# Two output projections taken one token stream at a time, with the residuals and norms placed behind them

## The chip, the cores and the metric

The kernel runs on one core of a Trainium2 chip. The metric is device microseconds (us) for one execution, taken as the median of three runs. Every run below is of the same program on the same inputs.

## The reference, cut to what matters

Two layers run over two token streams of 256 tokens each, context (`ctx`, stream 0) and latent (`x`, stream 1), with 1024 channels. Only the latent stream is wanted at the end, so the second layer gives no context output. Of each layer this much matters here:

```python
sh1, sc1, g1, sh2, sc2, g2 = split(silu(c) @ ada_w[layer] + ada_b[layer], 6)   # one set per stream
u = rms_norm(h, g_pre1) * (1 + sc1) + sh1
...                                               # three token mixers, each projected and gated
y = merged @ w_out                                # (256 tokens of a stream, 1024) @ (1024, 1024)
h = h + g1 * rms_norm(y, g_post1)
v = rms_norm(h, g_pre2) * (1 + sc2) + sh2
a = silu(conv3(v @ w_gate)) * (v @ w_val)         # 2816 channels
h = h + g2 * rms_norm(a @ w_ffn_out, g_post2)     # (256, 2816) @ (2816, 1024)
```

All values are float32.

## The kernel before, in words

**Products.** A float32 operand is split into a high part of a reduced format, which ScalarE writes with a cast, and a low part, the remainder, which VectorE or GpSimd writes with a subtraction. A product is then three matmuls: high x high, high x low, low x high. `weights` does it for a chunk of 128 x 1024 weights: one DMA of 512 KB from the SP queue into one of 5 buffers `raw`, one cast (`wh`, ScalarE), one subtraction (`wl`, VectorE), with 3 buffers each for `wh` and `wl`. The casts and subtractions stand in a block of high priority.

**Order.** A scheduler orders each engine's instructions at compile time, by priority (the order in which the code emits them) and by when its own model finds them ready. At run time each engine takes them strictly in that order, and a waiting instruction holds up all behind it.

**The output projections.** `outputs` computes `wo` (8 blocks of 128 input channels) and `fo` (22 blocks). A result of 128 tokens x 512 columns fills one PSUM bank. There are 3 banks `mm` and 5 banks `ps`. In layer 0, `outputs` takes the first 512 columns for both streams together, so that a chunk of weights serves 24 matmuls, and then the second 512 columns stream by stream, where each chunk serves 12 and is loaded and split again for the other stream. Stream 0's activations in front of `fo` are kept unsplit. `inner` splits one block of them when it is asked for: a cast into `ah` on ScalarE (L1170) and a subtraction into `al` on GpSimd (L1171), 128 x 256 each, two buffers each. In `outputs` it is asked once for each block and each half, and both tiles of 128 tokens use the answer.

**Behind the projections.** `post_half` takes the sum of squares of a bank (ScalarE, L383) and multiplies it with the gain row (VectorE, L436). `post_end` finishes the norm with two small GpSimd operations (L441, L378) and adds to the residual `h` (VectorE, L442). `norm_in` takes the next norm of `h`: a square pass (ScalarE), two small GpSimd operations, and a scaling of half the columns on ScalarE (L394) and half on VectorE (L395), into `hn`. `prenorm` then transposes `hn` by blocks of 128 (TensorE, L405, at high priority) and writes the split result `act`: high part on ScalarE (L409), the value again on VectorE (L411) and the remainder on VectorE or GpSimd (L412), two blocks to a call. All this is emitted after the whole projection.

**Modulation.** What the next steps need of `silu(c) @ ada_w` comes in two ways. `ada_dots` loads 512 KB of `ada_w` transposed and takes one product-and-sum on VectorE (L338, a "dot") for each stream wanted. `ada_units` does it on TensorE with narrow matmuls (L289), two units of 32 (64 instructions in the trace each) in either layer behind `wo`. In layer 0, the dots after `wo` are taken 2.7 for each of the FFN's blocks, and the rest beside the first half of `fo`.

Of the kernel before, what the change touches and what calls it, by code (L numbers as in the profile page):

```python
# [170 lines left out]
class Net:  # L171
# [102 lines left out]
    def ada_unit(self, l, cols, raw=None):  # L274

        nc = self.nc
        bank = self.ps()
        acc = bank[:, :P]
        nj = sum(n for _, n in cols) // P
        kb = 8 // nj  # L280
        for k2 in range(0, KD, kb):
            r = (raw or self.raw)(1024).rearrange("p (k c) -> p k c", k=kb)
            at = 0
            for c0, n in cols:
                nc.sync.dma_start(r[:, :, at:at + n], self.d["ada"][l, k2 * P:(k2 + kb) * P, c0:c0 + n].rearrange("(k p) c -> p k c", p=P))
                at += n
            for k in range(kb):
                for j in range(nj):
                    nc.tensor.matmul(acc[32 * j:32 * j + 32, :], self.scol[:, k2 + k, :], r[:, k, j * P:(j + 1) * P],  # L289
                                     start=k2 + k == 0, stop=k2 + k == KD - 1, skip_group_check=True)  # L290
            yield 460
        self.ada_turn(l, cols, bank)

# [32 lines left out]
    def ada_units(self, l, units):  # L326
        return chain(*(self.ada_unit(l, ((512 * i, 512),)) for i in units))

# [14 lines left out]
    def weights(self, key, urgent=True):  # L343
        nc = self.nc
        at, n = self.woff[key]
        raw = self.raw(n)
        nc.sync.dma_start(raw, self.d["wflat"][at:at + P * n].rearrange("(p f) -> p f", p=P))
        with self.tc.high_priority() if urgent else nullcontext():
            h = self.wp.tile([P, WCH], F32R, tag="wh", name=self.nm("wh"))[:, :n]
            nc.scalar.copy(h, raw)  # L350
            lo = self.wp.tile([P, WCH], F32R, tag="wl", name=self.nm("wl"))[:, :n]
            nc.vector.tensor_sub(lo, raw, h.bitcast(F32))  # L352
        return h, lo
# [43 lines left out]
    def prenorm(self, tp, l, ms, hn, k, boff, dst):  # L397

        nc = self.nc
        ps = self.ps().rearrange("p (i c) -> p i c", i=2)  # L400
        todo = [(m, g) for m in ms for g in hn]
        with self.tc.high_priority():
            for i, (m, g) in enumerate(todo):
                for t in range(2):
                    nc.tensor.transpose(ps[:, i, t * P:(t + 1) * P], hn[g][t][:, m * P:(m + 1) * P], self.ident)  # L405
        for i, (m, g) in enumerate(todo):
# [4 lines left out]
            nc.vector.tensor_scalar(t, ps[:, i], a, b, ALU.mult, ALU.add)  # L411
            (nc.gpsimd if i % 2 else nc.vector).tensor_sub(dst[1][:, m, c], t, dst[0][:, m, c].bitcast(F32))  # L412

    def norm_in(self, tp, l, g, hs, k, boff, dst):
        hn = [tp.tile([P, D], F32, tag="yg", name=self.nm("hn"), bufs=4) for _ in hs]
        for t in range(2):
            self.scaled(hn[t], self.rms(hn[t], hs[t]), hs[t])
        for m in range(0, KD, 2):
            self.prenorm(tp, l, (m, m + 1), {g: hn}, k, boff, dst)
# [18 lines left out]
    def post_end(self, s, yg, h):  # L438
# [3 lines left out]
        self.nc.vector.scalar_tensor_tensor(h, yg, self.rstd(ms, 1), h, ALU.mult, ALU.add)  # L442

    def outputs(self, key, nk, x, tp, gains, order, fill=iter(())):

        y, part = {}, {}

        def half(i, gs):
            for g in gs:
                y[g] = [(self.mm if 2 * i + t < MM_BANKS and g == order[0] and len(order) > 1 else self.ps)() for t in range(2)]  # L450
            last = nk - (4 if i and (gs[0] or nk == KD) else 0)
            for k in range(0, last, 2):
                w = self.weights((*key, i, k))
                if i == 0:
                    next(fill, None)
                for j in range(2):
                    for g in gs:
                        x_ = x(g, k + j)
                        for t in range(2):
                            self.tokens_proj(y[g][t], [a[:, t * P:(t + 1) * P] for a in x_], [a[:, 512 * j:512 * j + 512] for a in w], k + j == 0, k + j == nk - 1)  # L460
            ws = [(k, self.weights((*key, i, k))) for k in range(last, nk, 2)]
            for t in range(2 if ws else 0):
                for k, w in ws:
                    for j in range(2):
                        self.tokens_proj(y[g][t], [a[:, t * P:(t + 1) * P] for a in x(g, k + j)], [a[:, 512 * j:512 * j + 512] for a in w], False, k + j == nk - 1)
            for g in gs:
                for t in range(2):
                    self.post_half(tp, y[g][t], gains[g], i, *part[g, t])

        for g in order:  # L470
            for t in range(2):
                part[g, t] = self.st(2), tp.tile([P, D], F32, tag="yg", name=self.nm("yg"), bufs=4)
        half(0, order)
        for g in order:
            half(1, (g,))
        return part
# [810 lines left out]
```

## Time and profile before

| | |
|---|---|
| median of three runs | 1566.59 us (1565.92 to 1570.48) |
| the profiled execution | 1565.92 us, of which the span of instructions is 1564.1 us |
| mean granted TensorE clock | 0.991 |
| TensorE (PE) busy | 1485.0 us, 95% of the span |
| VectorE (DVE) busy | 1039.7 us, 66% |
| ScalarE (ACT) busy | 737.6 us, 47% |
| GpSimd (POOL) busy | 244.6 us, 16% |
| read from HBM | 225.06 MB, 145 GB/s over the span |

Times of rows count from the span's start. A busy TensorE need not be at its best pace, since matmuls overlap: a matmul with 512 columns lasts about 0.39 us, and the next one starts well before it ends. So the distance between starts is what counts, and a stage is read by how many matmuls it holds and how long it takes.

### The profile page before, as it was taken

What the parts mean: (1) busy time and instruction counts of PE and PEld (TensorE: products, weight loads), DVE (VectorE), ACT (ScalarE), POOL (GpSimd) and SP (SyncE); (2) the same over time, 40 slices, a digit from 0 to 9 for tenths busy, and PEclk for the clock granted to TensorE, in tenths of its full rate; (3) what the DMA queues carried; (4) which work ended last, traced back from release to release, by engine and by line L of the source; (5) the groups of instructions that cost most, each with busy time, mean ns of one, the idle gap of its engine ahead of it and who ended that gap; (6) DMA issues with size and microseconds to landing.
All of it is one profiled execution on the core that took longest, in us unless ns stands there. A gap on an engine that the chain in (4) does not pass through costs nothing.

```text
span 1564.1 us, 24165 instructions
## 1 busy us (share of the span) xinstructions
PE 1485.0 (95%) x9187; PEld 1275.2 (82%) x9187; DVE 1039.7 (66%) x1872; ACT 737.6 (47%) x1326; POOL 244.6 (16%) x335
## 2 busy tenths in 40 slices
PE   6999989999999998999999999899999989899998
PEld 5889867777777887888878886899997878699986
DVE  5546677778897448777776447646667797577754
ACT  3463334454454346332323346564456555455543
POOL 2101220101211223000000316401111123100000
PEclk9999999999999999999999999999999999899999
DMA  9331134423332356766665544422351234655553
GB/s 355 115 95 61 61 121 128 139 71 95 109 120 87 116 174 217 233 238 217 227 207 174 171 138 158 127 95 82 95 166 65 75 108 122 215 187 185 185 182 105
DMA packets 69717, 227.70 MB, mean 146 GB/s; under 512 B 7712, under 2 KB 8368, under 8 KB 69600
## 3 DMA queue, kind: packets, MB, share of 16 engines
q1 hardware_dynamic: 68000, 220.76, 43.4%
q0 software_dynamic: 1600, 5.39, 1.0%
q8 instruction: 72, 1.18, 0.3%
q14 instruction: 45, 0.37, 0.1%
HBM read 225.06 MB, written 1.06 MB: 145 GB/s over the span
## 4 chain that ended last, share of the span: by engine, by line
PE 62%; DVE 14%; issue 7%; DMA 7%; ACT 5%; POOL 4%; SPq 0%; POOLq 0%; ACTq 0%; DVEq 0%
PE mm L364 8%; PE mm L365 8%; PE mm L366 8%; DMA raw<-in_adat 6%; DVE wl L352 4%; PE ps L483 4%; PE ps L481 4%; PE ps L482 4%; DVE adot L338 3%; POOL st L378 2%; PE ps L366 2%; PE mm L579 2%; PE ps L364 2%; PE ps L365 2%; PE mm L580 2%
## 5 line engine op out<-in xcount | busy, mean ns | idle before, releaser
L352 DVE TENSOR_TENSOR wl<-raw,wh 128x1024 fp32r<-128x1024 f32 (+6 forms) x333 | 386.3, 1165 | 185.5 <-ACT wh L350 184.4
L350 ACT CAST wh<-raw 128x1024 fp32r<-128x1024 f32 (+6 forms) x333 | 320.1, 966 | 245.8 <-PE mm L365 102.6
L364 PE MATMUL mm<-act,wh 128*128 128x256 f32 (+1 forms) x1096 | 372.6, 340 | 5.4 <-ACT sig L978 2.0
L366 PE MATMUL mm<-act,wl 128*128 128x256 f32 (+1 forms) x1096 | 370.4, 338 | 3.4 <-DVE wl L352 3.4
L365 PE MATMUL mm<-act,wh 128*128 128x256 f32 (+1 forms) x1096 | 370.3, 338 | 0.2 <-POOL act L412 0.2
L364 PEld LDWEIGHTS mm<-act,wh 128*128 128x128 f32 x1096 | 210.2, 192 | 27.8 <-ACT wh L350 3.6
L366 PEld LDWEIGHTS mm<-act,wl 128*128 128x128 f32 x1096 | 210.1, 192 | 25.3 <-DVE wl L352 4.6
L365 PEld LDWEIGHTS mm<-act,wh 128*128 128x128 f32 x1096 | 210.3, 192 | 20.1 <-POOL act L412 0.4
L338 DVE CUSTOM_DVE_ANT_0 adot<-raw,srow,S 128x1024 bf16<-128x1024 f32 x104 | 134.2, 1291 | 73.6 <-DMA raw<-in_adat 69.0
L366 PE MATMUL ps<-act,wl 128*128 128x256 f32 (+1 forms) x328 | 109.5, 334 | 1.1 <-DVE wl L352 1.1
L364 PE MATMUL ps<-act,wh 128*128 128x256 f32 (+1 forms) x328 | 109.4, 333 | 0.0
L365 PE MATMUL ps<-act,wh 128*128 128x256 f32 (+1 forms) x328 | 109.3, 333 | 0.0
L483 PE MATMUL ps<-wh,al 128*128 128x512 f32 x198 | 78.8, 398 | 3.2 <-POOL al L1171 3.2
L579 PE MATMUL mm<-wh,act 128*128 128x272 f32 (+1 forms) x256 | 77.7, 303 | 1.3 <-ACT kb L795 1.3
L1047 ACT ACTIVATE ft<-ft 128x256 f32<-128x256 f32 (+1 forms) x47 | 23.7, 503 | 114.2 <-DVE ft L1045 90.5
L581 PE MATMUL mm<-wh,act 128*128 128x272 f32 (+1 forms) x256 | 76.9, 301 | 0.3 <-POOL act L412 0.3
L580 PE MATMUL mm<-wl,act 128*128 128x272 f32 (+1 forms) x256 | 76.8, 300 | 0.3 <-DVE wl L352 0.3
L1171 POOL TENSOR_TENSOR al<-ac,ah 128x256 fp32r<-128x256 f32 x44 | 41.4, 944 | 214.5 <-ACT ah L1170 214.3
L366 PEld LDWEIGHTS ps<-act,wl 128*128 128x128 f32 x328 | 62.7, 191 | 7.5 <-DVE wl L352 1.5
L365 PEld LDWEIGHTS ps<-act,wh 128*128 128x128 f32 x328 | 62.7, 191 | 6.0
L364 PEld LDWEIGHTS ps<-act,wh 128*128 128x128 f32 x328 | 62.8, 191 | 5.8
L378 POOL TENSOR_TENSOR st<-st,mhalf 128x1 f32<-128x1 f32 (+3 forms) x56 | 48.6, 868 | 95.9 <-DVE st L606 59.0
(300 smaller groups left out, 2812.4 us busy)
## 6 DMA issues: line engine op xcount, KB each, us to landing
raw<-in_wflat SPq DMA_DIRECT2D x253, 512.0 KB, 3.6
raw<-in_adat SPq DMA_DIRECT2D x80, 512.0 KB, 4.2
raw<-in_wflat SPq DMA_DIRECT2D x48, 256.0 KB, 2.6
araw<-in_ada SPq DMA_DIRECT2D x16, 512.0 KB, 7.5
raw<-in_ada SPq DMA_DIRECT2D x16, 512.0 KB, 4.1
raw<-in_wflat SPq DMA_DIRECT2D x8, 480.0 KB, 3.5
raw<-in_wflat SPq DMA_DIRECT2D x8, 408.0 KB, 3.4
raw<-in_wflat SPq DMA_DIRECT2D x8, 384.0 KB, 6.6
```

The source lines that it names most:

```text
L338: nc.vector.tensor_tensor_reduce(junk, r, rows[:, i], 1.0, self.S[l][:, L_AB + b:L_AB + b + 1], ALU.mult, ALU.add, self.MV[l][:, b, g:g + 1])
L350: nc.scalar.copy(h, raw)
L352: nc.vector.tensor_sub(lo, raw, h.bitcast(F32))
L364: self.nc.tensor.matmul(ps, a, xh(k), start=first and k == 0, stop=False)
L365: self.nc.tensor.matmul(ps, a, xl(k), start=False, stop=False)
L366: self.nc.tensor.matmul(ps, b, xh(k), start=False, stop=last and k == nk - 1)
L378: self.nc.gpsimd.tensor_tensor(r, ms, self.mhalf[:, :n], ALU.pow)
L481: self.nc.tensor.matmul(ps, xh, wh, start=first, stop=False)
L483: self.nc.tensor.matmul(ps, xl, wh, start=False, stop=last)
L579: nc.tensor.matmul(ps, uh[:, k, tt], h[:, c], start=k == 0, stop=False)
L580: nc.tensor.matmul(ps, uh[:, k, tt], lo[:, c], start=False, stop=False)
L581: nc.tensor.matmul(ps, ul[:, k, tt], h[:, c], start=False, stop=k == KD - 1)
```

## The change: what it does

- `outputs` now serves one stream for a call. Without `split`, the loop runs over pairs of blocks, inside it over the two column halves, inside that over the tiles of 128 tokens of the group `ts`, so four banks (or two) fill at once. The activation block is asked for (`x(k + j)`) in the innermost loop, for each half and each tile.
- In layer 0, `wo` runs for stream 0 and then stream 1; `fo` for stream 1 and then stream 0. All weights of `wo` and `fo` are thus loaded and split once for each stream. In layer 1, `wo` runs by tiles of 128 tokens, with split weights kept in a pool of their own for the second tile; `fo` keeps its order, with both tiles one after the other for the last two chunks of the second half.
- `renorm` replaces `norm_in`: the residual is added by halves of 512 columns, and ScalarE squares each half as it is done. It is called as soon as a tile of 128 tokens has both its halves. `normed` and `normed_next` emit the transposes of a stream in the midst of the next stream's products (`mid`), the early FFN blocks or the next layer's first projections, and no longer at high priority.
- In `prenorm` the remainder is always on VectorE; the second block of a call has its value taken again on ScalarE.
- `ada_units` is gone. In layer 0, dots are taken 2.4 for each FFN block, and the remaining ones beside the first 16 weight chunks of `fo` for stream 1. In layer 1, 16 dots (shift and scale of the second norm) go beside the first and the third merge, and 8 (the last gate) beside the FFN.
- The last residual is added and stored by halves of 512 columns.

```diff
+    def renorm(self, tp, s, yg, h):
+        q, ms = self.st(2), self.st(1)
+        self.post_end(s, yg, h, lambda i, c: self.square_sums(tp.tile([P, 512], F32, tag="ft", name=self.nm("jq"), bufs=2), h[:, c], q[:, i:i + 1]))
+        self.nc.gpsimd.tensor_scalar(ms, q[:, 0:1], q[:, 1:2], EPS, ALU.add, ALU.add)
+        hn = tp.tile([P, D], F32, tag="yg", name=self.nm("hn"), bufs=4)
+        self.scaled(hn, self.rstd(ms, 1), h)
+        return hn
...
+        for ts in tiles:
+            y = {(t, i): (self.mm if t == 0 else self.ps)() for t in ts for i in range(2)}
+            for k in range(0, nk, 2) if ts[0] == 0 else (nk - 2, *range(0, nk - 2, 2)):
+                for i in range(2):
+                    w = weights(i, k)
+                    for t in ts:
+                        for j in range(2):
+                            first, last = (k + j == 0, k + j == nk - 1) if ts[0] == 0 else (k + j == nk - 2, k + j == nk - 3)
+                            self.tokens_proj(y[t, i], [a[:, t * P:(t + 1) * P] for a in x(k + j)], [a[:, 512 * j:512 * j + 512] for a in w], first, last)
+                if mid and k == mid[0]:
+                    mid[1]()
+            for t in ts:
+                for i in range(2):
+                    end(t, i, y[t, i])
+                done(t, *yg[t])
...
-            ada = self.ada_dots(ap, [(l, b) for b in range(16, 40)], (0, 1)) if full else iter(())
+            ada = self.ada_dots(ap, [(l, b) for b in range(16 if full else 24, 40)], (0, 1) if full else (1,))
...
-            run(self.merge(l, sp, u, 2, yC, acc, q0, nq, mg))
+            run(self.beside(self.merge(l, sp, u, 2, yC, acc, q0, nq, mg), ada, 3000))
...
-        part = self.outputs((l, "wo"), KD, lambda g, k: (mg[0][:, k, at(g)], mg[1][:, k, at(g)]), fp, rows, groups, gains())
+        if full:
+            wo(0)
+            wo(1, mid=(KD - 4, partial(normed, 0)))
+        else:
+            with pool("wo", far) as wp:
+                wo(1, wp=wp, tiles=((0,), (1,)))
+                turn(0)
+                turn(1)
         mst.close()
-        ada = chain(self.ada_units(l + 1, range(2)), *(self.ada_dots(fp, [(l, b) for b in range(40, 48)] + [(l + 1, b) for b in range(8, 40 if g else 16)], (g,)) for g in range(2))) if full else self.ada_units(l, range(10, 12))
+        second = [(l, b) for b in range(40, 48)]
+        ada = chain(*(dots(second + [(l + 1, b) for b in range(24 if g else 16)], g) for g in range(2))) if full else dots(second, 1)
...
-                due += 2.7 if j < NF - 2 else 0
+                due += (2.4 if full else 0.5) if j < NF - 2 else 0
...
-        part = self.outputs((l, "fo"), NF, inner, fp, rows, groups[::-1], ada)
+            fo(partial(inner, 1), fp, lambda: rows[1], fill=lambda k: next(ada, None), done=renormed(1))
+            run(ada)
+            fo(partial(inner, 0), fp, lambda: rows[0], mid=(14, partial(normed_next, 1)), done=renormed(0))
...
+        def store(t, s, yg):
+            self.post_end(s, yg, hs[1][t], lambda i, c: nc.sync.dma_start(self.d["out"][t * P:(t + 1) * P, c], hs[1][t][:, c]))
+        fo(partial(inner, 1), fp, lambda: rows[1], split=4, done=store)
```

## Rows read from the trace of the kernel before

**Rows 1.** The page: busy time, share of the span and instructions by engine.

```profile
PE 1485.0 (95%) x9187; PEld 1275.2 (82%) x9187; DVE 1039.7 (66%) x1872; ACT 737.6 (47%) x1326; POOL 244.6 (16%) x335
```

**Rows 2.** Windows: length; busy PE, PEld, DVE, ACT, POOL; granted clock; DMA share, GB/s.

```profile
541.90:642.20 100.30, 92.93 (x658) 79.67 (x657) 67.28 (x98) 55.38 (x92) 25.50 (x30) 1.00 0.60 195
852.80:983.60 130.80, 126.93 (x548) 99.78 (x547) 66.93 (x72) 63.21 (x109) 49.23 (x60) 1.00 0.49 157
983.60:1008.80 25.20, 20.64 (x161) 20.44 (x160) 18.32 (x29) 15.83 (x30) 10.52 (x17) 0.93 0.37 108
220.00:440.00 220.00, 211.03 (x1201) 169.62 (x1200) 175.13 (x374) 108.09 (x217) 30.02 (x29) 0.99 0.36 114
1150.00:1222.00 72.00, 67.78 (x566) 59.93 (x565) 52.07 (x114) 43.97 (x90) 9.33 (x11) 1.00 0.29 91
1325.30:1351.80 26.50, 24.85 (x109) 20.00 (x112) 15.38 (x18) 11.59 (x19) 3.98 (x5) 0.94 0.59 182
1351.80:1372.20 20.40, 14.20 (x174) 12.30 (x175) 13.64 (x26) 11.10 (x19) 5.72 (x9) 0.75 0.74 257
1372.20:1495.60 123.40, 123.40 (x1030) 123.40 (x1030) 87.00 (x129) 69.65 (x108) 0.74 (x1) 1.00 0.58 184
636.00:656.00 20.00, 19.79 (x110) 17.40 (x111) 17.06 (x28) 7.61 (x12) 0.00 (x0) 1.00 0.83 281
```

**Rows 3.** TensorE in order of time, where layer 0's `wo` ends.

```profile
586.49 0.40 PE L481 MATMUL ps<-wh,mg 128*128 128x512 f32 x1
...
588.36 0.40 PE L483 MATMUL ps<-wh,mg 128*128 128x512 f32 x1
588.69 2.15 PE L289 MATMUL ps<-raw,scol 128*32 128x128 f32 x66
590.77 1.56 PE L405 MATMUL ps<-ident,hn 128*128 128x128 f32 x12
```

**Rows 4.** TensorE in order of time, where layer 1's `wo` ends.

```profile
1351.39 0.39 PE L483 MATMUL ps<-wh,mg 128*128 128x512 f32 x1
...
1359.00 2.82 PE L405 MATMUL ps<-ident,hn 128*128 128x128 f32 x12 [0.81 <-DVE hn L395]
...
1364.59 0.38 PE L364 MATMUL mm<-act,wh 128*128 128x256 f32 x1 [0.73 <-ACT wh L350]
```

**Rows 5.** TensorE in order of time, at the start of layer 1.

```profile
993.16 0.56 PE L405 MATMUL ps<-ident,hn 128*128 128x128 f32 x2 [4.56 <-ACT hn L394]
```

**Rows 6.** Groups of instructions by form over the span: busy us, mean ns.

```profile
L352 DVE TENSOR_TENSOR wl<-raw,wh 128x1024 fp32r<-128x1024 f32 x253 | 320.6, 1270 | 157.3 <-ACT wh L350 156.8
L350 ACT CAST wh<-raw 128x1024 fp32r<-128x1024 f32 x253 | 264.4, 1047 | 196.8 <-PE mm L365 76.1 <-PE ps L483 60.0 <-PE ps L365 34.9
L338 DVE CUSTOM_DVE_ANT_0 adot<-raw,srow,S 128x1024 bf16<-128x1024 f32 x104 | 134.2, 1291 | 73.6 <-DMA raw<-in_adat 69.0 <-DMA srow<-sdram 4.0
L409 ACT ACTIVATE act<-ps,MV,A 128x256 fp32r<-128x256 f32 x56 | 29.6, 563 | 32.2 <-PE ps L405 21.4 <-DVE nt L411 10.8
L1171 POOL TENSOR_TENSOR al<-ac,ah 128x256 fp32r<-128x256 f32 x44 | 41.4, 944 | 214.5 <-ACT ah L1170 214.3
L378 POOL TENSOR_TENSOR st<-st,mhalf 128x1 f32<-128x1 f32 x26 | 17.5, 675 | 6.1 <-DVE st L1224 4.2
L441 POOL TENSOR_SCALAR st<-st 128x1 f32<-128x1 f32 x12 | 6.9, 572 | 262.7 <-ACT junk L383 262.5
```

**Rows 7.** Line 1171 alone: duration min/median/max, and what waited for it.

```profile
L1171 POOL TENSOR_TENSOR al<-ac,ah x44: 722/738/1814, 614.8 to 981.0; 128x256 fp32r<-128x256 f32 x44
```

**Rows 8.** GpSimd in order of time, in the last part of layer 0's `fo`.

```profile
973.88 2.15 POOL L1171 TENSOR_TENSOR al<-ac,ah 128x256 fp32r<-128x256 f32 x2 [0.22 <-ACT ah L1170]
...
978.32 0.74 POOL L1171 TENSOR_TENSOR al<-ac,ah 128x256 fp32r<-128x256 f32 x1 [0.30 <-ACT ah L1170]
```

**Rows 9.** The page: DMA issues, KB each, us from issue to landing.

```profile
raw<-in_adat SPq DMA_DIRECT2D x80, 512.0 KB, 4.2
```

**Rows 10.** VectorE in order of time, at the end.

```profile
1558.51 1.28 DVE L442 SCALAR_TENSOR_TENSOR hL<-yg,st,hL 128x1024 f32<-128x1024 f32 x1 [0.47 <-POOL st L378]
```

More of the change, by code (lines that the diff above doesn't have):

```diff
@@ L341, in ada_dots, with weights @@
             yield 1500
[L343 removed]
+    def weights(self, key, urgent=True, pool=None):
         nc = self.nc
@@ L395, in scaled, with turned, prenorm @@
         self.nc.vector.tensor_scalar_mul(dst[:, D // 2:], src[:, D // 2:], r)
[L397 removed]
+    def turned(self, ps, ms, hn, t):
+        for i, m in enumerate(ms):
+            self.nc.tensor.transpose(ps[:, i * SEQ + t * P:i * SEQ + (t + 1) * P], hn[:, m * P:(m + 1) * P], self.ident)
+    def prenorm(self, tp, l, ms, hn, k, boff, dst, ps=None):
         nc = self.nc
[L400 removed]
         todo = [(m, g) for m in ms for g in hn]
[L402 removed]
+        if ps is None:
+            ps = self.ps()
             for i, (m, g) in enumerate(todo):
                 for t in range(2):
[L405 removed]
+                    self.turned(ps[:, i * SEQ:], (m,), hn[g][t], t)
+        ps = ps.rearrange("p (i c) -> p i c", i=2)
         for i, (m, g) in enumerate(todo):
@@ L410, in prenorm @@
             t = tp.tile([P, SEQ], F32, tag="nt", name=self.nm("nt"), bufs=2)
[L411 to L419, printed above, removed]
+            if i % 2:
+                nc.scalar.activation(t, ps[:, i], AF.Identity, bias=b, scale=a)
+            else:
+                nc.vector.tensor_scalar(t, ps[:, i], a, b, ALU.mult, ALU.add)
+            nc.vector.tensor_sub(dst[1][:, m, c], t, dst[0][:, m, c].bitcast(F32))
     def gate_rows(self, fp, l, k, g):
@@ L436, in post_half, with post_end @@
         self.nc.vector.tensor_mul(yg[:, c], y, gain[:, c])
-    def post_end(self, s, yg, h):
+    def post_end(self, s, yg, h, after):
         ms = self.st(1)
         self.nc.gpsimd.tensor_scalar(ms, s[:, 0:1], s[:, 1:2], EPS, ALU.add, ALU.add)
[L442 to L466, printed above, removed]
-                for t in range(2):
[L468 to L476, printed above, removed]
@@ L1148, in layer @@
         for g in groups:
-            for t in range(2):
-                self.post_end(*part[g, t], hs[g][t])
-            self.norm_in(fp, l, g, hs[g], "A2", 24, v)
             for j in early:
                 self.ffn_pair(l, fp, j, v, new(j), g * CTX, CTX, q0, True, j >= 2)
+                if not g and j == early[-2]:
+                    normed(1)
+        if not full:
+            for i, ps in enumerate(turns):
+                self.prenorm(fp, l, (2 * i, 2 * i + 1), {1: hn[1]}, "A2", 24, v, ps)
         due = 0
```

115 lines of the change are left out of this document (72 added, 43 removed).

## The prediction, made before the changed kernel was run

> **What bounds the kernel now.** I read the page first: TensorE is busy 95% of the span and every other engine 66% or less [rows 1]. So the time is a sum of matmuls at their best pace plus the places where TensorE runs short. I then cut the span into stretches and compared each with the pace of its matmuls. In the FFN of layer 1, TensorE is busy for the whole 123.4 us and starts 1030 matmuls of 256 columns, one each 0.120 us [rows 2]. In `wo`, matmuls of 512 columns start 0.234 us apart (nine from 586.49 to 588.36), a transpose takes 0.13 us (twelve in 1.56), and a narrow matmul of `ada_units` 0.033 us (66 in 2.15) [rows 3]. With these prices each stretch that the change touches has an ideal length, and what lies above it is what the change can win.
>
> Layer 0 from `wo` to the end of the early FFN blocks takes 100.3 us [rows 2]. It holds 192 products (44.9), 16 transposes of gains (2.1), 32 of `hn` (4.2), 288 FFN matmuls (34.5) and 128 narrow ones (4.2): 89.9. So 10.4 us are waits. The border to layer 1 takes 25.2 us [rows 2] for 144 matmuls (17.3) and 16 transposes (2.1), 5.8 us too many, of which one wait for `hn` is 4.56 us [rows 5]. In layer 1 the last product of `wo` starts at 1351.39, and the last transposes begin at 1359.00 [rows 4]; the granted clock of the stretch behind it is 0.75 [rows 2], a mean of the two levels 2.4 and 1.2 GHz. The FFN's 1056 matmuls would take 126.5 us back from 1495.6, so it starts in effect at 1369.1, 17.3 us after `wo`.
>
> **Layer 0, `wo` and early FFN.** `ada_units` goes (-4.2). The 16 weight chunks, where there were 12, cost 1.05 us of ScalarE and 1.27 us of VectorE each [rows 6] under 12 products (2.8 us): hidden. If both are lost or delayed, TensorE waits. Stream 0's chain from the last product to `hn` took 7.2 us in layer 1, from 1351.8 to 1359.0 [rows 4]. It now has three quarters of the second `wo` (17 us) to run in. Stream 1's has two FFN blocks (11.5 us). Ideal is 85.7, so the gain lies between 4.2 (all waits stay) and 14.6 (none). The normalization of a stream puts 12 ScalarE passes of 0.53 us [rows 6] beside the FFN's casts, so I leave 3.6 us of waits: **-11**.
>
> **Border to layer 1.** Without priority the transposes of stream 0 no longer stand in front of ready projections. That gives at most 5.8. The first V product then needs stream 0 whole: 12 ScalarE passes (6.4 us) against some 4 us of transposes and products, so I give back 2.3: **-3.5**, from -5.8 to 0.
>
> **Layer 1, `wo` and its norm.** The second tile's chain stays: 7.2 us. The first tile's transposes go into it. Then four pairs of blocks at three ScalarE passes each (1.6 us) feed the first FFN product; the last pair is ready 0.5 + 6.4 us later, at 14.1, and the 2.9 us of that product end with it: the FFN starts in effect at 11.2, not 17.3. At the clock that the idle time leaves [rows 2] I take -5. Against it, a chunk now serves six products (1.4 us) in the first tile. Eight chunks and four dots left over come to 6.3 MB (512 KB each [rows 9]). Part is loaded under the last merge, which leaves VectorE and the DMA room; I take +2, at worst +11. Sum **-3**, from -8 to +6.
>
> **Dots in layer 1.** 16 dots are 21 us of VectorE at 1.29 us [rows 6]. Both ends: 0, and 21 if each delays the attention's chain. The stretch of the first merge has VectorE busy 52 of 72 us and TensorE 67.8 of 72; layer 0 carries its dots in 220 to 440, with TensorE busy 211 of 220 [rows 2], no worse. **+3**. The 8 dots under the FFN are free: VectorE is busy 87 of 123.4 us there [rows 2], and TensorE never waits.
>
> **Layer 0, `fo`: the decisive part.** It takes 130.8 us now [rows 2]. Products are 264 for each stream, 61.8 us. Stream 1: 61.8 plus 2 for the gains, plus what the dots cost. For 16 chunks, weights and dot ask for 1.05 MB in 2.8 us, 373 GB/s, where the fastest stretch shown with these buffers moved 281 [rows 2]. VectorE needs 2.6 of the 2.8 us [rows 6]. Three chunks split ahead and five loaded cover most: +3, from 0 to +15 (all at 281 GB/s).
>
> Stream 0 is where I expect the loss. `x(k + j)` is called in the innermost loop, and for stream 0 that is `inner`, which emits a cast and a GpSimd subtraction at each call. Before, 22 blocks x 2 halves are 44 calls [rows 6]. After, 22 x 2 halves x 2 tiles are 88, each serving three products, 0.70 us. A subtraction takes 0.944 us in the mean [rows 6] and 0.738 in the median [rows 7]. Two of them that meet a VectorE subtraction take 2.15 us [rows 8], 0.67 more than two medians. So GpSimd needs 88 x 0.738 = 64.9 us at the least, 79.7 if each of the 22 chunks costs 0.67 once, and 83.1 at the mean, against 61.8 of products. I take the mean, since the stage it comes from has the same chunks and casts. In the same queue stand two tiles' norms of stream 1, each two L441 and two L378 (2.5 us): 88. At worst a weight cast (1.05 us) also delays a subtraction in each chunk: 111. The other operations of `prenorm` and its transposes fall into TensorE's waits. `fo` is 61.8 + 2 + 3 + 88 = 154.8: **+24**, from -2 (64.9, dots free) to +59 (111, dots at +15).
>
> The Trainium skill, on the page "SBUF — State Buffer" (section "SBUF: two separate sides"), says that GpSimd shares a port pair with VectorE, as an exclusive lock: a VectorE operation with two SBUF inputs and a GpSimd operation that reads SBUF block one another for the whole instruction. By that rule each chunk would cost a whole `wl`. The trace shows a little over half (0.67 of 1.27 us).
>
> **The end.** Two half additions in place of one of 1.28 us [rows 10], each followed by its store. The last store starts as late as before: 0. FFN 0 with 40 dots in place of 45: 0.
>
> **Sum.** -11 - 3.5 - 3 + 3 + 24 = +9.5 against the profiled execution's 1565.92 us (the median is 0.7 us above it): **1575 us**.
>
> **Rivals.** *The subtractions hide* (faster). GpSimd keeps its median, 64.9 us for 88, and no norm stands in its way. Then `fo` takes 131.7, +0.9, and the rest wins 14.5: 1552. It decides as soon as a subtraction comes under 0.70 us in effect. For it: in the first half of `fo` most are at the median. Against it: there one `wl` comes with each 24 products, here one with each 12. Chance 0.20.
>
> *Gains and loss cancel.* GpSimd stands at 79.7 and hides the norms: `fo` +15.6, in all +1, 1567. The pairs of [rows 8] speak for just this price. Chance 0.20.
>
> *A whole `wl` each time* (slower). Each chunk costs 1.27 us: 64.9 + 27.9 + 5 = 97.8, `fo` +33.8, in all 1585. Against it, the 2.15 us of a pair. Chance 0.12. This is what the exclusive lock on the Trainium skill's page "SBUF — State Buffer" would do here.
>
> *Loads bind* (slower). Every load beside a dot goes at 281 GB/s: +12 more in `fo` of stream 1, +9 more in layer 1's `wo`: 1596. For it, no stretch with five buffers is faster. Against it, up to eight chunks lie ready at the start. Chance 0.08.
>
> My forecast has the other 0.40, with a range of its own from 1571 to 1585.
>
> **The numbers.** About 0.3% (4.7 us) is what a measurement of this kernel tells from no change. Slower: 0.40 + 0.12 + 0.08 = 0.60. Within: 0.20. Faster: 0.20. The range reaches from the first rival to beyond the last, 1551 to 1600; below and above it I leave 0.1 each.
>
> **What would show it.** The successor of L1171 has 88 instructions, most with VectorE's `wl` beside them. In `fo` of stream 0, TensorE's third product waits for `al` in most groups, GpSimd is busy over 80% and the stage takes 85 to 95 us. Behind either `wo`, the wait for `hn` is gone in layer 0 and the FFN starts some 5 us sooner in layer 1. At the border no wait of 4 us for `hn` stands in front of ready projections. The prediction is wrong if GpSimd isn't what TensorE waits for there, if the layer 0 join wins nothing, or if the attention of layer 1 grows by more than 5 us.

## The result, and the profile after

The changed kernel takes **1604.79 us** (median of four runs, 1600.85 to 1608.21) against 1567.82 for the kernel before in the same comparison: ratio 1.024, 95% interval 1.0223 to 1.0256. The forecast was 1575 with a range to 1600. The direction was right, the size was not. The profiled execution took 1603.0 us with a span of 1601.2, so 37.1 us more than the span of 1564.1 before; the sum of the prediction had been 9.5.

The page's line of engines answers to [rows 1]: TensorE's share falls by two points, and every other engine is far from full.

```profile
PE 1495.9 (93%) x8927; PEld 1266.4 (79%) x8927; DVE 1078.5 (67%) x1938; ACT 785.5 (49%) x1433; POOL 259.0 (16%) x353
```

Taking the starts of TensorE's first or last instruction of each part in the two traces gives a ledger. All figures are us of the two profiled executions; the last column is the prediction's term.

| stretch | before | after | change | forecast |
|---|---|---|---|---|
| start to the last product with `yC` of layer 0 | 541.6 | 544.1 | +2.4 | 0 |
| from there to the first product of `fo` of layer 0 | 311.2 | 310.3 | -0.9 | -11 |
| `fo` of layer 0 | 130.5 | 165.3 | **+34.8** | +24 |
| border, to the first V product of layer 1 | 25.5 | 22.6 | -2.9 | -3.5 |
| layer 1 to its last product with `yC` | 316.2 | 320.7 | +4.5 | +3 |
| from there to the first product of its `fo` | 171.4 | 171.5 | +0.2 | -3 |
| `fo` of layer 1 and the end | 67.7 | 66.7 | -1.1 | 0 |
| sum | 1564.1 | 1601.2 | +37.0 | +9.5 |

The +2.4 in the first row isn't explained by any step of the change. In the experiments below, nearly all of which leave the code of that stretch as it is in the changed kernel, it ends anywhere from 540.6 to 544.2, so it lies within what executions differ by. The second row varies too: the seven experiments with the same code there show 308.7 to 314.2. So the -0.9 says only that the 11 us are missing.

So the loss is `fo` of layer 0, as forecast, but it is 11 us bigger, and the gains around both `wo` that were to pay for part of it are missing: 10 us in layer 0 and 3 in layer 1. Windows of the changed kernel (columns as in [rows 2]): `fo` of stream 1, `fo` of stream 0, and the stretch in front of layer 1's `wo`.

```profile
854.00:921.00 67.00, 64.29 (x276) 50.70 (x274) 45.24 (x56) 28.25 (x33) 0.86 (x2) 1.00 0.79 264
921.00:1020.00 99.00, 79.31 (x280) 44.86 (x280) 41.22 (x43) 62.89 (x137) 81.88 (x93) 0.98 0.37 117
...
1354.00:1372.00 18.00, 10.38 (x80) 9.32 (x78) 14.75 (x28) 6.75 (x14) 9.88 (x9) 0.89 0.77 246
```

Stream 0's first product starts at 919.60, so stream 1 takes 65.2 us with its dots, 1.6 under its price (66.8), and stream 0 takes 100.1 and not 88. From 921 on GpSimd is busy 83% of the time, not all of it. The groups by form over the span show where GpSimd's idle time comes from (they answer to the line of 44 in [rows 6]):

```profile
L1207 POOL TENSOR_TENSOR al<-ac,ah 128x256 fp32r<-128x256 f32 x88 | 81.2, 933 | 25.8 <-ACT ah L1206 14.0 <-DVE act L399 9.8 <-PE mm L495 1.8
...
L495 PE MATMUL ps<-wh,al 128*128 128x512 f32 x176 | 72.1, 410 | 15.7 <-POOL al L1207 15.7
...
L1206 ACT CAST ah<-ac 128x256 fp32r<-128x256 f32 x88 | 33.6, 403 | 31.9 <-POOL al L1207 21.5 <-PE ps L494 10.4
```

One subtraction takes 0.933 us; 0.944 was taken. But GpSimd waits for ScalarE's cast (14.0 us), and the cast waits for GpSimd (21.5) and for TensorE (10.4): a ring in which each waits for the next. One turn of it, from the timeline of stream 0's `fo`, which repeats every 4.31 us (wh at 964.14, then at 968.45):

```profile
964.14 1.04 ACT L328 CAST wh<-raw 128x1024 fp32r<-128x1024 f32 x1
...
964.31 0.75 POOL L1207 TENSOR_TENSOR al<-ac,ah 128x256 fp32r<-128x256 f32 x1 [0.16 <-ACT ah L1206]
...
965.09 0.71 ACT L1206 CAST ah<-ac 128x256 fp32r<-128x256 f32 x2
...
965.21 1.23 DVE L330 TENSOR_TENSOR wl<-raw,wh 128x1024 fp32r<-128x1024 f32 x1 [3.08 <-ACT wh L328]
...
965.57 2.90 POOL L1207 TENSOR_TENSOR al<-ac,ah 128x256 fp32r<-128x256 f32 x3 [0.50 <-ACT ah L1206]
...
967.05 0.41 ACT L1206 CAST ah<-ac 128x256 fp32r<-128x256 f32 x1 [1.26 <-POOL al L1207]
...
967.08 0.50 PE L495 MATMUL ps<-wh,al 128*128 128x512 f32 x1 [0.80 <-POOL al L1207]
...
968.13 0.41 ACT L1206 CAST ah<-ac 128x256 fp32r<-128x256 f32 x1 [0.67 <-PE ps L494]
...
968.45 1.05 ACT L328 CAST wh<-raw 128x1024 fp32r<-128x1024 f32 x1
...
969.52 1.22 DVE L330 TENSOR_TENSOR wl<-raw,wh 128x1024 fp32r<-128x1024 f32 x1 [3.08 <-ACT wh L328]
...
969.87 1.46 POOL L1207 TENSOR_TENSOR al<-ac,ah 128x256 fp32r<-128x256 f32 x1 [0.52 <-ACT ah L1206]
```

GpSimd is busy 0.75 + 2.90 = 3.65 us of the turn, and 0.66 us it waits: 0.16 behind one cast, 0.50 behind the cast that stood after the weight cast. There are two `ah` and two `al`, so the cast at 967.05 could start only when the subtraction two calls back had read its buffer. TensorE's 12 products need 2.8 us of the 4.31.

The other two losses stand in the lists of waits (total, times, longest). Around layer 0's `wo`, 545 to 556:

```profile
PE ps L493 <- ACT grow L409: 3.3, 1, 3.3
```

And in front of layer 1's, 1355 to 1375:

```profile
ACT mg L1007 <- POOL acc L1005: 11.2, 8, 3.5
PEld mm L493 <- ACT wh L328: 7.6, 1, 7.6
PE mm L493 <- ACT wh L328: 7.3, 1, 7.3
```

The rows of gains, turned ahead of `wo`, hold the PSUM banks until ScalarE copies them, and `wo` waits 3.3 us. In layer 1 the first weight cast of `wo` is 7.3 us late. Behind layer 0's `wo`, TensorE in order of time waits for splits of FFN weights, and for the second stream's last norm:

```profile
605.27 0.39 PE L342 MATMUL mm<-act,wh 128*128 128x256 f32 x1 [0.70 <-ACT wh L328]
...
608.16 0.58 PE L344 MATMUL mm<-act,wl 128*128 128x256 f32 x1 [2.38 <-DVE wl L330]
...
609.64 2.82 PE L378 MATMUL ps<-ident,hn 128*128 128x128 f32 x12 [0.48 <-ACT hn L372]
```

### The profile page after: what moved, and what is told of

It reads as the page before. It is cut to its first block, busy times and chain, and to the rows that moved or that the text cites. A ratio compares the mean times of both kernels' runs of the same rounds, so it can differ in the third digit from the quotient of the medians.

```text
span 1601.2 us, 23987 instructions
## 1 busy us (share of the span) xinstructions
PE 1495.9 (93%) x8927; PEld 1266.4 (79%) x8927; DVE 1078.5 (67%) x1938; ACT 785.5 (49%) x1433; POOL 259.0 (16%) x353
## 3 DMA queue, kind: packets, MB, share of 16 engines
HBM read 238.17 MB, written 1.06 MB: 149 GB/s over the span
## 5 line engine op out<-in xcount | busy, mean ns | idle before, releaser
L330 DVE TENSOR_TENSOR wl<-raw,wh 128x1024 fp32r<-128x1024 f32 (+5 forms) x348 | 399.0, 1152 | 178.8 <-ACT wh L328 176.6
L328 ACT CAST wh<-raw 128x1024 fp32r<-128x1024 f32 (+5 forms) x348 | 335.9, 970 | 248.9 <-PE mm L343 99.8
L315 DVE CUSTOM_DVE_ANT_0 adot<-raw,srow,S 128x1024 bf16<-128x1024 f32 x128 | 164.5, 1285 | 81.8 <-DMA raw<-in_adat 75.4
L495 PE MATMUL ps<-wh,al 128*128 128x512 f32 x176 | 72.1, 410 | 15.7 <-POOL al L1207 15.7
L1207 POOL TENSOR_TENSOR al<-ac,ah 128x256 fp32r<-128x256 f32 x88 | 81.2, 933 | 25.8 <-ACT ah L1206 14.0
L421 POOL TENSOR_SCALAR st<-st 128x1 f32<-128x1 f32 x12 | 4.2, 351 | 431.2 <-ACT junk L361 431.0
```

Of the source, the lines that this page charges most:

```text
L315: nc.vector.tensor_tensor_reduce(junk, r, rows[:, i], 1.0, self.S[l][:, L_AB + b:L_AB + b + 1], ALU.mult, ALU.add, self.MV[l][:, b, g:g + 1])
L495: self.nc.tensor.matmul(ps, xl, wh, start=False, stop=last)
L1207: nc.gpsimd.tensor_sub(lo, a[k][0], h.bitcast(F32))
```

## The experiments

Each kernel is the changed one with the edit shown, or builds on the one named. Medians stand with the ratio to the kernel before on the same chip and its 95% interval; the first four kernels, the next four, the next four and the last three ran on one chip each. Lengths of stretches are those of the profiled executions. The kernel before gave 1565.69 to 1567.21 us on these four chips, so kernels from different chips are best compared by their ratios. Where two intervals overlap (`kept` with `kept_late`, `kept_urgent`, `kept_dotsc` or `kept_own`; `best` with `best_whole`, `best_sq64` or `best_mid`), the total alone doesn't tell them apart, and the reading rests on the waits and stretches named.

| kernel | median us | ratio to before |
|---|---|---|
| ring | 1580.93 | 1.0095 (1.0072 to 1.0118) |
| half | 1581.69 | 1.0096 (1.0067 to 1.0126) |
| kept | 1566.29 | 1.0001 (0.9988 to 1.0015) |
| vec | 1598.34 | 1.0209 (1.0187 to 1.0231) |
| kept_late | 1563.94 | 0.9981 (0.9969 to 0.9993) |
| kept_urgent | 1570.88 | 1.0024 (1.0006 to 1.0042) |
| kept_dotsc | 1562.85 | 0.9982 (0.9968 to 0.9995) |
| kept_short | 1561.79 | 0.9972 (0.9961 to 0.9982) |
| kept_own | 1562.85 | 0.9984 (0.9969 to 0.9998) |
| best | 1558.35 | 0.9953 (0.9940 to 0.9965) |
| best_norm | 1566.07 | 1.0003 (0.9995 to 1.0012) |
| best_whole | 1562.80 | 0.9972 (0.9961 to 0.9983) |
| best_sq64 | 1559.68 | 0.9949 (0.9930 to 0.9968) |
| best_mid | **1556.23** | 0.9926 (0.9907 to 0.9946) |
| best_sqv | 1567.23 | 1.0000 (0.9983 to 1.0018) |

### What holds stream 0's `fo`: four kernels

**ring.** All 88 calls stay, but their results go in turn into 22 pairs of buffers, those of stream 1, and no longer into two.

```diff
+        asked = []
         def inner(g, k):
...
-            h, lo = (fp.tile([P, CTX], F32R, tag=n, name=self.nm(n), bufs=2) for n in ("ah", "al"))
+            h, lo = a[len(asked) % NF][1:]
+            asked.append(k)
```

> The 88 casts and 88 GpSimd subtractions of stream 0's fo stay, but their results go into 22 pairs of buffers (those of stream 1, free by then) and no longer into two, so that no cast waits for products. Theory A (a loop: the chunk's 4.30 us are 3.65 us of GpSimd plus 0.65 us in which GpSimd waits for ScalarE, whose casts wait for the two buffers and for the weight cast in front of them): the 0.65 us go, 14 us over 22 chunks, total 1589 to 1593. Theory B (GpSimd's own time is the limit, as the prediction had it): no change, 1601 to 1608. Theory C (the stage is held by its weight loads or by VectorE, not by the subtractions): no change, and products wait for weights.

Measured: 1580.93, 24 us less than the changed kernel and 8 below theory A's range. From 948 on GpSimd now runs without a gap; this is its timeline in the middle of the stage, where 31 subtractions stand in one unbroken row:

```profile
954.31 30.76 POOL L1210 TENSOR_TENSOR al<-ac,al 128x256 fp32r<-128x256 f32 x31
```

Between 960 and 972 a chunk takes 3.76 us (TensorE's groups of 12 products start at 960.52, 964.28, 968.04), 0.94 us a subtraction, the mean that the prediction had used (over the whole row of 31 it is 0.99). A chunk of 3.76 us is 0.55 less than 4.31, 12 us in 22 chunks. `fo` as a whole is 21.4 us shorter (143.9). The rest goes with a head start: 20 of the 88 subtractions run before 918, under stream 1's products, where the two buffers had allowed two in the changed kernel. Theory B falls, and A has the mechanism, with that head start left out of its sum.

**half.** The split is asked for once per chunk, for both token tiles, as in the kernel before.

```diff
                     w = weights(i, k)
+                    xs = [x(k + j) for j in range(2)]
                     for t in ts:
...
-... [a[:, t * P:(t + 1) * P] for a in x(k + j)] ...
+... [a[:, t * P:(t + 1) * P] for a in xs[j]] ...
```

> The splits of stream 0 are asked for once per chunk and not once per token tile: 44 casts and 44 subtractions as in the kernel before, two buffers each. Theories A and B: GpSimd has 1.9 us of work under 2.8 us of products, the stage falls from 99 to 62 to 67 us, total 1568 to 1573. Theory C (weight loads or VectorE hold the stage): 1600 to 1608.

Measured: 1581.69, where theories A and B said 1568 to 1573. Both miss here. GpSimd has half the work, yet a chunk takes 3.03 us (in ScalarE's timeline below the same cast comes back after 3.04) and `fo` 141.8 us. ScalarE's casts wait for TensorE:

```profile
967.56 0.41 ACT L1207 CAST ah<-ac 128x256 fp32r<-128x256 f32 x1 [0.98 <-PE ps L495]
968.25 0.41 ACT L1207 CAST ah<-ac 128x256 fp32r<-128x256 f32 x1 [0.29 <-PE ps L495]
968.57 1.05 ACT L328 CAST wh<-raw 128x1024 fp32r<-128x1024 f32 x1
970.60 0.41 ACT L1207 CAST ah<-ac 128x256 fp32r<-128x256 f32 x1 [0.98 <-PE ps L495]
```

Both buffers serve the chunk in work, so nothing of the next chunk can be split before the second tile's products of this one. The steady loss is 22 x 0.21 = 4.6 us of the 12.4 by which this `fo` exceeds that of `kept`; the rest seems to arise where stream 1's norms stand in ScalarE's queue (925 to 940) and there is no split ahead to live on, which no run tested by itself.

**kept.** Each block is split once, for both halves and both tiles.

```diff
-            h, lo = (fp.tile([P, CTX], F32R, tag=n, name=self.nm(n), bufs=2) for n in ("ah", "al"))
+            h, lo = a[k][1:]
+            if k in asked:
+                return h, lo
+            asked.append(k)
```

> Each of stream 0's 22 blocks is split once and kept for both halves and both tiles: 22 casts and 22 subtractions. Theories A and B: as with 44, the stage at 62 to 66 us, total 1567 to 1572, and no faster than with 44 by more than 3 us, since GpSimd is hidden in both. Theory C: 1600 to 1608. If the norms of stream 1 in GpSimd's queue are what costs at the start of the stage, this one is faster than the 44 by up to 4 us.

Measured: 1566.29, 38.5 us less, no different from the kernel before. `fo` takes 129.4 us (before 130.5), and in 921 to 986 TensorE is busy for 64.98 of 65 us.

**vec.** The 88 subtractions on VectorE.

```diff
-            nc.gpsimd.tensor_sub(lo, a[k][0], h.bitcast(F32))
+            nc.vector.tensor_sub(lo, a[k][0], h.bitcast(F32))
```

> All 88 subtractions stay, on VectorE in place of GpSimd: 0.42 us each, with the weight's 1.22 us 2.9 us a chunk against 2.8 us of products. Theory A: the loop over ScalarE stays, but without GpSimd in it a chunk takes 2.9 to 3.3 us, stage 65 to 73 us, total 1571 to 1580. Theory B: the same, 1571 to 1575. Theory C (VectorE or the loads hold the stage): slower than after, over 1605.

Measured: 1598.34, only 6.5 us less and outside the ranges of all three theories. A subtraction takes 0.42 us there instead of 0.93, but a chunk still takes 4.01 us (its weight casts start at 958.96, 962.98 and 966.98). The list of waits of this kernel, in 945 to 1000, shows the same ring with VectorE in GpSimd's place:

```profile
ACT ah L1206 <- DVE al L1207: 11.5, 15, 1.1
...
ACT ah L1206 <- PE ps L494: 7.3, 13, 0.6
PE ps L495 <- DVE al L1207: 7.3, 13, 0.6
```

Together the four settle it. With two buffers a chunk takes 4.31 us with GpSimd and 4.01 with VectorE, which subtracts in less than half the time; with 22 pairs and GpSimd 3.76; with one split per block 2.82. Over the whole of `fo` (165.3, then 143.9 in `ring`, 129.4 in `kept`) the buffers are worth 21.4 us, head start included, and GpSimd's own time the other 14.5; in a chunk of the middle it is 0.55 and 0.94. The Trainium skill, on the page "Perfetto Trace Analysis" (section "Optimization Strategy"), says that the same gap coming back on the engine that should be full can mean that there is no buffer for the next tile; the 0.80 us in front of the product at 967.08, once in every 4.31 us, is such a gap. The runs bear this out in part: with 22 pairs of buffers a turn is 0.55 us shorter, but TensorE still waits 0.71 us for `al` in front of the product at 960.52, once in every 3.76 us, and that gap is GpSimd's own time.

### Layer 1's dots and its `wo`: three kernels

All three build on `kept`. There layer 1's `wo` starts 8.45 us after the last product with `yC` (0.69 before).

**kept_dotsc.** The second eight dots beside attention C.

```diff
-... self.beside(self.merge(l, sp, u, 1, yA, acc, q0, nq), ada if full else iter(())), (0.92, 0.34)[l])
+... self.beside(self.merge(l, sp, u, 1, yA, acc, q0, nq), ada), (0.92, 0.34)[l])
```

> On top of the kernel that keeps the splits (1566.3 us): the second eight dots of layer 1 run beside attention C and the second merge, and none is left for the third merge. Theory H (the dots left over for the end of the third merge stand in VectorE's order ahead of the steps that feed ScalarE, and hold wo of layer 1 by 7 us): wo starts 6 to 8 us sooner, attention C grows by 0 to 4 us, total 1558 to 1563. Theory I (a dot costs the same wherever it stands, VectorE being full): 1564 to 1568.

Measured: `wo` starts 2.66 us after `yC`, and attention and merges grow by 1 to 2 us (169.5 here, from the first scores of attention A on; 166.4 to 168.7 in the kernels with the dots where the change put them, 169.0 to 170.7 in all with this edit). Total 3.4 us less by the medians. The price does depend on where a dot stands, so theory I falls.

**kept_short.** The dots stay, but read 64 columns.

```diff
-                nc.vector.tensor_tensor_reduce(junk, r, rows[:, i], 1.0, ...
+                w = 64 if l and b < 40 and streams == (1,) and b >= 24 else D
+                nc.vector.tensor_tensor_reduce(junk[:, :w], r[:, :w], rows[:, i, :w], 1.0, ...
```

> On top of the kernel that keeps the splits (1566.3 us): the 16 dots beside layer 1's attention and merges sum over 64 of their 1024 columns (the rest of these sums is left out); their loads stay. Theory H (VectorE's time and order): the wait in front of layer 1's wo goes (7 us) and the attention's growth (4 to 6 us) too, total 1554 to 1558. Theory J (the loads of the dots, which stand ahead of wo's chunks in SyncE's queue, hold wo): the wait in front of wo stays, total 1562 to 1566.

Measured: the attention's growth goes (from the first V product to the last with `yC`: 323.0 in `kept` and 319.2 to 323.2 in the other kernels with these dots, 317.5 here, 316.2 before), but `wo` still starts 7.32 us late. So theory H holds for the attention and theory J in front of `wo`. SyncE's timeline of this kernel shows what is there:

```profile
1316.49 3.88 SPq L312 DMA_DIRECT2D raw<-in_adat  x3
1320.73 5.35 SPq L325 DMA_DIRECT2D raw<-in_wflat  x5
```

The first chunk of `wo` is asked for at 1320.73, 0.65 us before the last `yC` product; before the change that was 1316.45, 8.6 us ahead of it.

**kept_own.** The dots stay whole, with five buffers of their own.

```diff
-            r = self.raw(D)
+            r = pool.tile([P, D], F32, tag="draw", name=self.nm("draw"), bufs=5) if l and 24 <= b < 40 else self.raw(D)
```

> On top of the kernel that keeps the splits (1566.3 us): the 16 dots of layer 1 stay where the change put them, but load into five buffers of their own and not into the five shared with the weights. Theory M (the dots' rows hold all five shared buffers until VectorE comes to them, so that the first chunk of layer 1's wo is asked for too late): the wait in front of wo shrinks from 8.4 us to 2 to 4, total 1560 to 1563. Theory H (VectorE's time and order in front of wo): the wait stays at 7 to 8 us, total 1565 to 1568.

Measured: `wo` starts 3.39 us after `yC`, total 1562.85, though the stretch up to attention A's first scores is 2.9 us longer here (154.5 to 157.4), for which no cause was sought. Theory M holds: five rows for dots fill the five buffers that the weights use too, VectorE takes them one between two steps of the merge, and SyncE, in order, can't ask for `wo` before.

### Layer 0's `wo`, and the gains together: eight kernels

**kept_late.** On `kept`, rows of gains behind the second chunk of their stream's `wo`.

```diff
-        for g in groups:
-            rows[g] = self.gate_rows(fp, l, "G1", g)
+        def gains(g, k):
+            if k == 2 and g not in rows:
+                rows[g] = self.gate_rows(fp, l, "G1", g)
...
+... fill=partial(gains, g) ...
```

> On top of the kernel that keeps the splits (1566.3 us): the rows of gains are turned behind the second chunk of their stream's wo, as before the change, and not ahead of wo. Theory D (the rows, which wait on ScalarE behind the last merge, hold four PSUM banks that wo's products need: a gap of 3.7 us in layer 0): the gap goes, total 1562 to 1564. Theory E (ScalarE's queue is late for wo's weight casts just as well): the wait moves to wh, total 1565 to 1568.

Measured: the wait of 3.3 us is gone, and from layer 0's last `yC` product to the last product of `wo` it takes 49.1 us, where `kept` takes 53.4 and the changed kernel 51.9. Up to `fo` the gain over `kept` is 3.3 us (312.05 to 308.73); total 2.4 us less. Theory D holds.

**kept_urgent.** On `kept`, weight casts of the first two FFN blocks with priority.

```diff
-self.ffn_pair(l, fp, j, v, new(j), g * CTX, CTX, q0, True, j >= 2)
+self.ffn_pair(l, fp, j, v, new(j), g * CTX, CTX, q0, True)
```

> On top of the kernel that keeps the splits (1566.3 us): the casts of the weights of the first two early FFN blocks of each stream are also given priority over the normalization in front of them. Theory F (the waits at the join behind layer 0's wo, 3 to 4 us, are for weight splits that stand behind the renormalization in the queues of ScalarE and VectorE): 2 to 4 us less, 1562 to 1564. Theory G (both queues are full there, so what the splits gain the normalization loses): 1565 to 1568.

Measured: 4.6 us more. TensorE's waits for `wl` shrink from 3.5 us to 0.9, but 1.8 us for `hn` come in their place, and the stretch is 2.6 us longer, 314.6. Theory F falls; the total lies above G's range too.

**best** puts `kept`, the late rows and the dots beside attention C together.

> Kept splits, rows of gains behind the second chunk of wo, and layer 1's second eight dots beside attention C, all three together. If the two small gains (3 us and 4 us against the kernel before) lie in different stages and add: 1558 to 1561, ratio to the kernel before 0.994 to 0.997, faster than before by more than it is uncertain. If one takes the other's place: 1562 to 1565.

Measured: 1558.35; the small gains add, and the interval is clear of the kernel before.

**best_norm.** On `best`, the shifts as before the change.

```diff
-            if i % 2:
-                nc.scalar.activation(t, ps[:, i], AF.Identity, bias=b, scale=a)
-            else:
-                nc.vector.tensor_scalar(t, ps[:, i], a, b, ALU.mult, ALU.add)
-            nc.vector.tensor_sub(dst[1][:, m, c], t, dst[0][:, m, c].bitcast(F32))
+            nc.vector.tensor_scalar(t, ps[:, i], a, b, ALU.mult, ALU.add)
+            (nc.gpsimd if i % 2 else nc.vector).tensor_sub(dst[1][:, m, c], t, dst[0][:, m, c].bitcast(F32))
```

> On top of the three together: the elementwise part of the normalization as before the change (all shifted tiles on VectorE, every other subtraction on GpSimd), so that ScalarE has one pass per block and not one and a half. Theory K (ScalarE is the engine that the join behind layer 0's wo and layer 1's first FFN blocks run at, busy without a break from 588 to 609): 2 to 5 us less than the three together. Theory L (VectorE or GpSimd bind just as much there, since they meet on their common port): the same, or up to 4 us more.

Measured: 7.7 us more in the median and 3.9 in the profiled execution, where the stretch between `yC` and `fo` of layer 0 is 4.9 us longer. Its list of TensorE's waits from 586 to 612 begins:

```profile
PE mm L343 <- POOL act L396: 3.5, 2, 2.5
```

TensorE waits for GpSimd's subtraction. Theory K falls, and the loss is above what L allowed; this part of the change is a gain of 4 to 8 us.

**best_whole.** On `best`, layer 1's `wo` without the split by 128 tokens.

```diff
-                wo(1, wp=wp, tiles=((0,), (1,)))
+            wo(1)
```

> On top of the three together: wo of layer 1 by both column halves of both token tiles at once, as in layer 0, and not by 128 tokens. If the split by tiles hides the first tile's chain, as the prediction had it: 4 to 8 us more than the three together (the FFN starts later by that). If ScalarE's passes are what the FFN waits for, or the starved first tile costs what the chain saves: within 2 us.

Measured: 4.4 us more. From the last product of `wo` to `fo` it takes 142.9 us instead of 137.9, while `wo` starts 2.7 sooner. So the split by tiles wins 5.0 us behind `wo` and pays about half of that at its start.

**best_sq64** and **best_sqv.** On `best`, square sums behind layer 0's `wo` over 64 columns; and those of the renormalization on VectorE.

```diff
-        self.nc.scalar.activation(junk, x, AF.Square, scale=D ** -0.5, accum_out=out)
+        w = 64 if getattr(self, "few", False) else x.shape[1]
+        self.nc.scalar.activation(junk[:, :w], x[:, :w], AF.Square, scale=D ** -0.5, accum_out=out)
```
```diff
-lambda i, c: self.square_sums(..., h[:, c], q[:, i:i + 1])
+lambda i, c: self.nc.vector.tensor_tensor_reduce(..., h[:, c], h[:, c], 1.0 / D, 0.0, ALU.mult, ALU.add, q[:, i:i + 1])
```

> On top of the three together (1558.4 us): the square sums behind layer 0's wo, 16 passes of ScalarE of some 0.55 us over 512 columns, read 64 columns each (the rest of these sums is left out). Theory N (behind wo the second stream's chain runs over ScalarE, and it is this chain that the first FFN blocks and their weight splits wait for): the stretch from the last merge to fo gets 3 to 6 us shorter, total 1552 to 1556. Theory O (VectorE or GpSimd hold the chain and the splits there): under 1.5 us.

> On top of the three together (1558.4 us): the square sums of the renormalization (four a stream, wherever a stream is renormalized) on VectorE in place of ScalarE. Theory N: 1 to 3 us less, 1555 to 1557. Theory O: 1 to 4 us more, as with the shifts on VectorE and GpSimd.

Measured: with most of the squares gone the stretch is no shorter (309.2 against 307.3); TensorE's waits from 586 to 608 are others (2.6 us for `hn`, 1.7 for `wh`) and sum to as much. Moved to VectorE, the squares make it 3.9 us longer and the border 4.9, more than theory O allowed. Theory N falls: time on ScalarE alone isn't what holds the join, and VectorE has none to spare.

**best_mid.** On `best`, stream 0 turned and shifted one pair of chunks earlier.

```diff
-            wo(1, mid=(KD - 4, partial(normed, 0)))
+            wo(1, mid=(KD - 6, partial(normed, 0)))
```

> On top of the three together (1558.4 us): stream 0's 16 blocks are turned and shifted one pair of chunks earlier in stream 1's wo. Theory P (their 12 ScalarE passes and the last weight casts collide with stream 1's chain): the same stretch gets 2 to 4 us shorter, total 1554 to 1557. Theory Q (stream 0's own chain is not ready so early, and TensorE waits for it in order): 0 to 4 us longer, 1558 to 1562.

Measured: 1556.23, the fastest of all, 0.7% under the kernel before and 3% under the changed one. The first 48 FFN products, from 592.40 to 598.24, now run without a wait (0.124 us apart); in `best` 1.14 us for `wl` and 0.3 for a shifted tile stood there. The stretch is 1.8 us shorter and the total 2.1. That points to theory P at its lower end; but `best_whole`, with the code of `best` there, already differs from it by 1.6 in that stretch, so only the two waits that are gone, 1.4 us, are shown. What stays are the waits for the next block's weights, of which the list for 586 to 608 shows:

```profile
PE mm L344 <- DVE wl L330: 2.4, 1, 2.4
PE mm L342 <- ACT wh L328: 0.7, 1, 0.7
PE ps L378 <- ACT hn L372: 0.3, 1, 0.3
```

## Why the prediction was right and wrong

Of the 27.5 us by which the profiled executions differ more than forecast, 10.8 lie in `fo` of layer 0 and 10.1 at layer 0's `wo`. Two steps failed, and each came out dearer than forecast.

**`fo` of stream 0, forecast +24, came +34.8. This is the first step that failed.** The place was right, and so was the cause, the 88 calls: 88 subtractions of 0.933 us (0.944 taken), TensorE's third product waits for `al`, and GpSimd is over 80% busy. The step "GpSimd needs ... 83.1 at the mean" treated a sum of busy time as the length of a stage, and gave 88 us where 100.1 came. It asked what stands beside each subtraction on VectorE, and not what must happen between two of them. With two buffers, a cast follows the subtraction and the products of two calls before, and a weight cast of 1.05 us stands in ScalarE's order between two casts. That ring takes 4.31 us a chunk where the forecast had 4.00. The sentence on the worst case ("a weight cast also delays a subtraction in each chunk") named half of it, priced it at the whole 1.05 us, and left it at the edge of the range; 0.66 came. The rows were there to see it: in [rows 8] a wait for `ah` of 0.22 and 0.30 us stands in front of the subtractions.

**The rivals.** "A whole `wl` each time" (1585) pointed the same way, and its 97.8 us for stream 0 is near the 100.1 only by luck: it has no ring in it, and its price for a `wl` is too high. The subtraction that meets a `wl` takes 1.46 us, 0.72 more than the median, and the `wl` beside it stays at 1.23. The times of the turn shown above say why: a `wl` runs from 969.52 to 970.74, and the subtraction that starts at 969.87 ends at 971.33, 0.59 us behind it. So the subtraction lost what was left of the `wl`, 0.87 us, less 0.15; in 52 of 53 such cases it went like this (last section). The Trainium skill's page "SBUF — State Buffer" (section "SBUF: two separate sides") says that whichever of the two starts first holds the shared ports for its whole instruction, and that the other blocks. The trace agrees. The prediction compared the loss with the whole `wl` (0.67 of 1.27 us, "a little over half"), and not with what was left of it when the subtraction came. "Loads bind" didn't occur: stream 1 came in under its price, and of its products TensorE waits 0.8 us for `wl` and never for a load itself.

**Layer 0, `wo` and early FFN, forecast -11, came -0.9. This is the second step that failed,** and by the prediction's own sign of being wrong: the join won nothing. The term at fault is the 3.6 us of waits. The removed work went, and new waits stand in its place. 3.3 us are the rows of gains, a moved step for which the prediction counted no wait: it had not named the PSUM banks that they hold, nor ScalarE's queue behind the third merge. More is lost at the join: from 596.18, where the last product of `wo` is through, to 612.12 TensorE does 53 FFN matmuls and 16 transposes, 8.4 us at the prices of [rows 2, 3], in 15.9 us. That is 7.5 us for this one place, twice the 3.6 allowed for the whole stretch: 5.0 us are waits, and 1.3 more are the transposes at the lower clock (last section). At 638 to 640 stand another 1.9 us, for `wh` and `ft`. The estimate that stream 1's chain hides in "two FFN blocks (11.5 us)" was short: from 596.18 to the turning of its last `hn` at 609.64 it takes 13.5 us and not 7.2, and ScalarE's and VectorE's orders there have casts and subtractions of weights and stream 0's last shifts between its steps. Shifting stream 0 earlier takes 1.4 us of waits away. Why the rest stays is open: neither priority for the weights, nor fewer squares on ScalarE, nor the shifts or squares on other engines gave it back.

**Layer 1's `wo` and norm, forecast -3, came +0.2.** The two terms were right in sign. Behind `wo` -7.6 came for -5. In front +7.8 came for "+2, at worst +11". Its reason, 6.3 MB to be moved, was not the cause: the dots hold the five buffers, and the load of `wo` is asked for too late.

**The dots beside attention** cost 4.5 us for +3, and 64 columns in place of 1024 take nearly all of that away: VectorE's time. **The border** gained 2.9 for 3.5. **Stream 1's `fo`** and **the end** were right within 1.6 us.

## What to carry to other kernels

A helper that splits its operand at each call is priced by its calls, and a loop over tiles put inside them doubles them: keep the result, or give it buffers. The length of a stage with two buffers is the time once around its ring, casts, subtraction and products with all that stands in order between them; the busiest engine's sum is only a lower bound. And a step that borrows a shared pool (PSUM banks, load buffers) ahead of the main work delays that work by as long as it takes to give them back, however little time it takes itself.

## What the runs showed of the hardware

A GpSimd subtraction and a VectorE subtraction, both with two inputs in SBUF, took turns in the three traces looked at. In layer 0's `fo` of the kernel before, the changed one and `ring`, 53 subtractions into `al` start while a `wl` is being written; 52 of them end 0.58 to 0.61 us behind that `wl`, whether 0.19 or 1.17 us of it were left, where one alone takes 0.74. The other one started 4 ns behind its `wl`, and there it was the `wl` that took 0.6 us longer. In the changed kernel the `wl` always came first, and only GpSimd lost (0.72 us). In `ring`, where GpSimd had no gaps, a `wl` often found a subtraction running and lost too (0.27 us of 0.42 left): its groups over 948 to 1000 show 1.42 us in the mean for `wl` and 1.06 for the subtractions.

```profile
L1210 POOL TENSOR_TENSOR al<-ac,al 128x256 fp32r<-128x256 f32 x48 | 48.9, 1058 | 0.0
...
L330 DVE TENSOR_TENSOR wl<-raw,wh 128x1024 fp32r<-128x1024 f32 x15 | 21.3, 1419 | 20.0 <-ACT wh L328 20.0
```

In `ring`'s chunks of 3.76 us, subtractions that meet no `wl` start 0.70 us after one another, and the next one after the subtraction that meets it starts 1.67 us later. So an estimate from these starts is that four without a `wl` beside them would take 2.8 us, as long as the chunk's products: the 0.94 us that `ring` still loses in a chunk would then be this turn-taking. No run tested it.

After the 2.38 us wait at 605 the twelve transposes took 2.82 us where 1.56 is their time at 2.4 GHz (granted clock 1.00) [rows 2, 3]. TensorE was busy for 1.34 us of 605 to 609; the granted clock from 609.6 to 612.2 is 0.50, the level of 1.2 GHz, and from 613.6 on it is 0.98. So those waits cost 1.3 us more behind them.
